# Meta tokens left out behind the mLSTM's state, groups of 256 in the second layer, and a pair's two states block-diagonal in one matrix

## The chip, the cores and the metric

The kernel runs on one core of a Trainium2 chip. The metric is the device time of one execution in microseconds (us). The kernel before takes 3135.82 us (median of three runs, 3132.17 to 3137.7).

## The reference

A trunk of two layers works on 1040 tokens of width 1024: 16 learned meta tokens are set ahead of 1024 input tokens. Each layer is norm, token mixer, residual add, norm, squared-ReLU MLP (1024 to 4096 to 1024), residual add. Layer 0 mixes with a gated DeltaNet, layer 1 with an mLSTM. The output drops the 16 meta tokens again.

The mLSTM has 8 heads, with keys and queries of 64 and values of 128. Cut to what the kernel computes for one head and one chunk of tokens:

```
num   = ec * (q @ C) + (exp(decay) * (q @ k.T)) @ v     # and the same with v = 1 for den
C     = ecl * C + (kw * k).T @ v                        # state that the next chunk reads
h     = num / max(|den|, 1);  out = rms_norm(h) * sigmoid(o)
```

A meta token's `num`, its output gate, its share of the output product and its MLP in layer 1 reach no output. Only its key and value do, through the state C.

## The kernel before, in words

Tokens lie along the free axis: hT is 8 tiles of 128 features by 1040 tokens. Every dense product goes through mm3 (L114 to L117), three matmuls of one kind (fp32r, one record each in the profile): high part of weights by high part of activations, high by low, low by high. A stationary weight tile of 128 by 128 meets a moving tile of G = 260 tokens, four groups to 1040.

The second layer has four stages.

- **mLSTM projections.** MLSTM.proj (L1414) makes q, k, v0, v1, so0 and so1 of a pair of heads: six weight tiles, four groups, 24 matmuls each. There are four pairs.
- **mLSTM mix.** MLSTM.mix (L1445) is a generator. While pair p is projected, mix of pair p-1 is woven in: Ctx.weave steps it once at each yield of the dense work, which comes after every 12 matmuls. Tokens are nine chunks: the 16 meta tokens (number 8 in the code, first in the loop) and eight of 128. The products here are of plain fp32, two records to a matmul; only the transposes are one record. Per chunk and head the mix forms q times state (L1536, 64 partitions deep, one head's 129 columns), scores times values (L1539) and the state's update (L1550, 64 columns of weights, output on 64 of 128 partitions). The state of a pair is one tile, head 0 on partitions 0 to 63, head 1 on 64 to 127. ScalarE scales q times state by ec (L1545), VectorE adds scores times values (L1546), ScalarE squares and sums (L1547), VectorE forms the new state (L1555). For the meta chunk there are small scores (L1485), a small value product (L1539, 16 by 16) and small transposes (L1505) as well. PSUM has two buffers for L1536 and L1539, and one for L1550.
- **Output product.** MLSTM.out (L1589) adds the output product to hT in four groups of 260 (ps_mo); the last pair's mix is woven into it.
- **MLP.** Up (Strassen-like products of seven operands, ps_up, groups of 260) writes its activations to DRAM; Down (ps_dn) reads them back and adds to hT. In layer 1 the first half of Down is one group of 504 tokens, the second two of 260 (REAL, L39). ToOut.write (L1259) transposes 4 blocks of 126 tokens and 5 of 104 and writes them out; the last write ends the kernel.

The order of instructions on each engine is set by the framework's scheduler from the program's order; in the profile the two heads' products of a chunk stand apart, with dense matmuls between them.

Of the kernel before, what the change touches and what calls it, by code (L numbers as in the profile page):

```python
# [15 lines left out]
P = 128  # L16
# [21 lines left out]
ALL = [[(0, G), (G, G)], [(2 * G, G), (3 * G, G)]]  # L38
REAL = [[(META, HALF - META)], ALL[1]]  # L39
# [11 lines left out]
def pair(pool):  # L51
    return tuple(pool.tile([P, 2, HALF], F32R, tag=t, name="act_" + t) for t in ("hi", "lo"))
# [869 lines left out]
class Norm:  # L922


    def __init__(self, c, pool, nw, ss=None):
        self.c, self.nc, self.pool, self.nw = c, c.nc, pool, nw
        self.ss = pool.tile([P, T], F32, tag="ss", name="ss") if ss is None else ss
# [13 lines left out]

    def sums(self, hf):

        nc, c = self.nc, self.c
        pc = c.pq.tile([P, 512], F32, tag=c.pq_tag, name="ps_nrm")[:NT, :2 * G // NT]
        for i in range(2 * G // NT):
            t0 = hf * HALF + i * NT
            nc.tensor.matmul(pc[:, i:i + 1], self.ss[:, t0:t0 + NT], c.ones[:, 0:1], start=True, stop=True)
        nc.scalar.activation(c.rt, pc, AF.Sqrt, scale=1.0 / D, bias=c.eps[:NT])
        nc.vector.reciprocal(c.rt, c.rt)  # L950
        self.summed = hf

    def rms(self, hf):

        nc, c = self.nc, self.c
        if self.summed != hf:
            self.sums(hf)
        yield
        r = self.pool.tile([P, 2, G], F32, tag="r", name="nr", bufs=1)
        dg = r.rearrange("p a b -> p (a b)")[:NT].rearrange("p (a b) -> p a b", b=NT)  # L960
        nc.vector.tensor_tensor(dg, bc(c.ident[:NT, :NT], 1, 2 * G // NT), bc(c.rt, 2, NT), op=ALU.mult)
        yield
        for g in range(2):
            pr = c.pq.tile([P, 512], F32, tag=c.pq_tag, name="ps_nrm")[:, :G]
            nc.tensor.matmul(pr, c.ones[:NT], r[:NT, g], start=True, stop=True)
            nc.scalar.copy(r[:, g], pr)
        return r

    def apply(self, hf, pool):
# [6 lines left out]
        ts = slice(hf * HALF, (hf + 1) * HALF)  # L976
# [11 lines left out]
    def combine(self, hf, pool):  # L988
# [8 lines left out]
        ts = slice(hf * HALF, (hf + 1) * HALF)  # L997
        for j in range(KT // 2):
            b, t = (x.rearrange("p (a b) -> p a b", b=G) for x in self.stages())
            hi, lo = (pool.tile([P, 7, G], F32R, tag=n, name=n) for n in ("xhi", "xlo"))  # L1000
            for k, out in ((j, b[:, 0:4:3]), (j + 4, b[:, 1:3])):
                nc.vector.scalar_tensor_tensor(out, c.hT[:, k, ts].rearrange("p (a b) -> p a b", b=G),
                                               self.nw[:, k:k + 1], r, op0=ALU.mult, op1=ALU.mult)
# [13 lines left out]
class Up:  # L1017
# [47 lines left out]
    def evac(self, i, hs, name, ps, tmp):  # L1065
# [3 lines left out]
        def tile(pool, n):  # L1069
            return pool.tile([P, 2, G], F32, tag=n, name="up_" + n)[:, hs]  # L1070
# [28 lines left out]
    def run(self, jobs):  # L1099
# [4 lines left out]
        for ji, (i, parts, before) in enumerate(jobs):  # L1104
# [4 lines left out]
            for u, (name, xi) in enumerate(self.ORDER):  # L1109
# [7 lines left out]
                ps = self.ps.tile([P, 2, 512], F32, tag="pu", name="ps_up")[:, :, :G]  # L1117
# [8 lines left out]
class Down:  # L1126


    def __init__(self, c, w_down, acts, after, spans):
        self.c, self.nc, self.w, self.acts, self.after, self.spans = c, c.nc, w_down, acts, after, spans  # L1130
        self.a, self.pools, self.next = {}, [], []
# [4 lines left out]
    def fetch(self, j):  # L1136
        st = self.c.row(j % 2, "a_st")
# [3 lines left out]
    def load(self, j):  # L1141
# [3 lines left out]
        hi, lo = self.a[j] = pair(self.pools[j // HB % 2])  # L1145
# [6 lines left out]
    def tiles(self, b, dd, parts, last):  # L1152
# [33 lines left out]
def mlp(c, w_up, w_down, norm, spans, sides, xa, st, acts, after, closed):  # L1186


    down = Down(c, w_down, acts, after, spans)
# [49 lines left out]
class ToOut:  # L1239

    TILES = ((126, 4), (104, 5))

# [16 lines left out]
    def write(self, d, hf):  # L1259
        nc, c = self.c.nc, self.c  # L1260
        w, m = self.TILES[hf]
        t0 = (META, HALF)[hf]
        yield
        for i0 in range(0, m, 4):
            n = min(4, m - i0)
            pt = c.pj.tile([P, 4, P], F32, tag="pj", name="ps_fin")[:w, :n]
            for i in range(n):
                a = t0 + (i0 + i) * w
                nc.tensor.transpose(pt[:, i], c.hT[:, d, a:a + w], c.ident)
            ot = self.pool.tile([P, 4, P], F32, tag="ot", name="ot")[:w, :n]  # L1270
            nc.scalar.copy(ot, pt)
            r0 = t0 - META + i0 * w
            nc.sync.dma_start(out=self.out[r0:r0 + n * w, d * P:(d + 1) * P].rearrange("(i p) f -> p i f", p=w),
                              in_=ot)


class MLSTM:

# [19 lines left out]
    def dense(self, whl, g, m=P):  # L1298
        ps = self.c.pj.tile([P, 512], F32, tag="pj", name="ps_m")[:m, :G]
        gs = slice((g % 2) * G, (g % 2 + 1) * G)  # L1300
# [35 lines left out]
    def gates(self):  # L1336
# [34 lines left out]
        nc.scalar.activation(kw, kw, AF.Exp)  # L1371
        nc.vector.tensor_tensor(cm, pc[:META, 2, :, 0], self.lw[:META, :, 2 * GC], op=ALU.add)
# [15 lines left out]
        self.num = g1.tile([P, GC + 1, 2, P + 1], F32, name="num")  # L1388
        nc.gpsimd.memset(self.num[:, GC], 0.0)

    def decay(self, p, hf):
# [7 lines left out]
        if hf == 0:  # L1399
            E0 = self.g2.tile([META, 2, META], F32, tag="E0", name="E0")  # L1400
            for j in range(2):
                nc.sync.dma_start(out=E0[:, j], in_=md[2 * p + j, 2 * GC, :META].partition_broadcast(META))
                nc.vector.scalar_tensor_tensor(E0[:, j], E0[:, j], self.lw[:META, 2 * p + j, 2 * GC:],
                                               c.mneg[:META, :META], op0=ALU.add, op1=ALU.add)
            nc.scalar.activation(E0, E0, AF.Exp)
# [6 lines left out]
        return (E, E0) if hf == 0 else (E,)  # L1412

    def proj(self, p, s, streams, normed):  # L1414
# [8 lines left out]
        for i, ((name, col, sc), gs) in enumerate(work):  # L1423
# [12 lines left out]
            for g in gs:  # L1436
                ps = yield from self.dense(whl, g)
                dst = s[name][:, g // 2, (g % 2) * G:(g % 2 + 1) * G]
# [6 lines left out]
    def mix(self, p, s):  # L1445
        nc, c, g1, g2 = self.nc, self.c, self.g1, self.g2
        E, E0 = s["E"]
        E = [E, self.decay(p, 1)[0]]
# [10 lines left out]
        for hf in range(2):  # L1459
# [3 lines left out]
            for ci, cc in enumerate(chunks(hf)):  # L1463
                m = P if cc < 2 * GC else META
# [3 lines left out]
                nc.vector.tensor_tensor(kw[:m, ci], pt[:m, 0].rearrange("p (h d) -> p h d", h=2),  # L1468
                                        bc(self.kw[:m, 2 * p:2 * p + 2, cc], 2, 64), op=ALU.mult)
                nc.scalar.copy(V[:m, ci, :, 0:P], pt[:m, 1:3])  # L1470
                yield

        def scores(hf):
# [8 lines left out]
            if hf == 0:  # L1482
                pk = [self.pp.tile([META, META], F32, tag="pp", name="mpk0") for _ in range(2)]
                for j, sl in enumerate(self.HEADS):
                    nc.tensor.matmul(pk[j], part("k", 2 * GC, META)[sl], part("q", 2 * GC, META)[sl],  # L1485
                                     start=True, stop=True)
                for j in range(2):
                    nc.vector.tensor_tensor(E0[:, j], E0[:, j], pk[j], op=ALU.mult)
                yield

        def gated(hf):
            n, o0 = GL[hf], GO[hf]
            for j in range(2):
                og = g1.tile([P, XW], F32, tag="mog", name="mog")[:, :n]
                w = c.mlstm_nw[:, 2 * p + j:2 * p + j + 1]
                so = s[f"so{j}"].rearrange("p a b -> p (a b)")[:, hf * XW:hf * XW + n]
# [3 lines left out]
                nc.vector.scalar_tensor_tensor(og[:, o0:], pt.rearrange("p c t -> p (c t)"), w, so[:, o0:],  # L1500
                                               op0=ALU.mult, op1=ALU.mult)
                yield
                if hf == 0:
                    pt = self.pp.tile([P, META], F32, tag="pp", name="mpo3")
                    nc.tensor.transpose(pt, n2[:META, 2 * GC + j, 0:P], c.ident[:META, :META])  # L1505
                    nc.vector.scalar_tensor_tensor(og[:, :META], pt, w, so[:, :META], op0=ALU.mult, op1=ALU.mult)
                    yield
                if p < self.NH // 2 - 1:
                    nc.sync.dma_start(out=self.dram["o"][2 * p + j, :, hf * XW:hf * XW + n], in_=og)
                    continue  # L1510
                for oh in range(hf + 1) if hf else range(2):
                    a, b = max(hf * XW, oh * HALF), min(hf * XW + n, (oh + 1) * HALF)
                    if a >= b:
                        continue
                    hi, lo = (t[:, j, a - oh * HALF:b - oh * HALF] for t in self.o[oh][p])
                    og_ = og[:, a - hf * XW:b - hf * XW]
                    nc.scalar.copy(hi, og_)
                    nc.vector.tensor_tensor(lo, og_, hi.bitcast(F32), op=ALU.subtract)
# [5 lines left out]
        for hf in range(2):  # L1524
            V = self.V[hf]
            nch = GC + (hf == 0)
# [228 lines left out]
```

## Time and profile before

| what | us |
|---|---|
| median of three runs | 3135.82 |
| the profiled execution | 3135.46 |
| its span | 3133.5 |
| TensorE busy in it | 3056.0 |
| VectorE busy | 1944.4 |
| ScalarE busy | 1482.9 |
| from the first ps_m to the first ps_up of layer 1 (mLSTM) | 1883.5 to 2413.7 |
| from there to the first ps_dn of layer 1 (Up) | 2413.7 to 2759.8 |
| from there to the end (Down, writing) | 2759.8 to 3133.5 |

Matmuls are pipelined, so the time of one is longer than the distance between two; what a matmul costs is read from the starts of its neighbours. PEld is the loading of weights, which can run beside a matmul.

### The profile page before, as it was taken

How to read it: one execution, taken by the hardware profiler on the slowest of the kernel's cores; microseconds unless marked ns; L12 is line 12 of the kernel's file. 1: busy time of each engine (PE TensorE's matmuls, PEld its weight loads, DVE VectorE, ACT ScalarE, POOL GpSimd, SP SyncE). 2: the span in 40 equal slices, each digit the busy share in tenths (PEclk: the TensorE clock that was granted, in tenths of full speed). 3: DMA queues.
4: the chain of work that ended last, by engine and by line, in shares of the span. 5: the costliest groups of instructions: out<-in, count | busy, mean ns of one | idle time of the engine just before them, and what ended most of it. 6: DMA issues, size and time to landing. Idle time of an engine off the chain costs nothing.

```text
span 3133.5 us, 65556 instructions
## 1 busy us (share of the span) xinstructions
PE 3056.0 (98%) x26788; PEld 2910.6 (93%) x26788; DVE 1944.4 (62%) x4483; ACT 1482.9 (47%) x3390; POOL 303.6 (10%) x536
## 2 busy tenths in 40 slices
PE   7999999999999998999999999999999899999999
PEld 7899998999999998999999999899889899989998
DVE  6866777787776578665544554323358876654443
ACT  5666667766655345555311124433444555531112
POOL 1333332232322000000000000000000000000000
PEclk9999999999999999999999999999999999999999
DMA  4233333233335723433423222111222443342323
GB/s 106 80 84 88 88 91 89 82 102 93 88 105 161 227 81 114 129 119 106 141 92 102 89 68 69 51 56 58 67 80 82 122 123 110 117 146 76 100 89 101
DMA packets 402220, 310.97 MB, mean 99 GB/s; under 512 B 30175, under 2 KB 366432, under 8 KB 401920
## 3 DMA queue, kind: packets, MB, share of 16 engines
q1 hardware_dynamic: 366320, 272.69, 29.6%
q10 hardware_dynamic: 35600, 34.10, 3.2%
q8 instruction: 211, 3.46, 0.5%
q14 instruction: 89, 0.73, 0.1%
HBM read 248.11 MB, written 58.62 MB: 98 GB/s over the span
## 4 chain that ended last, share of the span: by engine, by line
PE 83%; DVE 7%; DMA 5%; ACT 2%; issue 1%; POOL 1%; SPq 0%; POOLq 0%; DVEq 0%; ACTq 0%
PE ps_dn L115 8%; PE ps_dn L116 8%; PE ps_dn L117 8%; PE ps_up L115 5%; PE ps_up L116 5%; PE ps_up L117 5%; PE ps_in L115 5%; PE ps_in L117 5%; PE ps_in L116 5%; PE ps_m L115 3%; PE ps_m L117 3%; PE ps_m L116 3%; PE ps_out L115 2%; PE ps_out L117 2%; PE ps_out L116 2%
## 5 line engine op out<-in xcount | busy, mean ns | idle before, releaser
L116 PE MATMUL ps_dn<-act_lo,whi 128*128 128x260 f32 (+1 forms) x1792 | 535.2, 299 | 0.0
L115 PE MATMUL ps_dn<-act_hi,whi 128*128 128x260 f32 (+1 forms) x1792 | 534.8, 298 | 0.4 <-DVE up_c L1073 0.3
L117 PE MATMUL ps_dn<-act_hi,wlo 128*128 128x260 f32 (+1 forms) x1792 | 533.2, 298 | 0.0
L115 PE MATMUL ps_up<-xhi,uop 128*128 128x260 f32 x1792 | 512.3, 287 | 19.9 <-DVE up_u L1073 7.8
L117 PE MATMUL ps_up<-xhi,uop 128*128 128x260 f32 x1792 | 509.5, 285 | 6.6 <-DVE uop L1062 6.6
L116 PE MATMUL ps_up<-xlo,uop 128*128 128x260 f32 x1792 | 511.3, 286 | 0.7 <-DVE xlo L1010 0.7
L134 ACT CAST whi<-wraw 128x1024 fp32r<-128x1024 f32 (+1 forms) x248 | 255.8, 1032 | 511.7 <-PE ps_dn L116 363.8
L115 PE MATMUL ps_in<-act_hi,whi 128*128 128x264 f32 (+1 forms) x1536 | 451.7, 294 | 2.2 <-ACT sz L525 1.2
L117 PE MATMUL ps_in<-act_hi,wlo 128*128 128x264 f32 (+1 forms) x1536 | 448.9, 292 | 0.0
L116 PE MATMUL ps_in<-act_lo,whi 128*128 128x264 f32 (+1 forms) x1536 | 446.7, 291 | 0.0
L1166 DVE TENSOR_TENSOR hT<-hT,ps_dn 128x260 f32<-128x260 f32 (+1 forms) x448 | 203.9, 460 | 327.1 <-PE ps_dn L117 326.7
L135 DVE TENSOR_TENSOR wlo<-wraw,whi 128x1024 fp32r<-128x1024 f32 (+1 forms) x248 | 299.9, 1209 | 149.3 <-ACT whi L134 146.8
L115 PEld LDWEIGHTS ps_up<-xhi,uop 128*128 128x128 f32 x1792 | 341.5, 191 | 25.1 <-issue 6.7
L117 PEld LDWEIGHTS ps_up<-xhi,uop 128*128 128x128 f32 x1792 | 342.1, 191 | 7.9 <-DVE uop L1062 7.8
L115 PEld LDWEIGHTS ps_dn<-act_hi,whi 128*128 128x128 f32 x1792 | 336.9, 188 | 11.6 <-DVE up_c L1073 0.5
L117 PEld LDWEIGHTS ps_dn<-act_hi,wlo 128*128 128x128 f32 x1792 | 337.7, 188 | 10.7
L116 PEld LDWEIGHTS ps_dn<-act_lo,whi 128*128 128x128 f32 x1792 | 336.9, 188 | 10.4
L116 PEld LDWEIGHTS ps_up<-xlo,uop 128*128 128x128 f32 x1792 | 342.5, 191 | 1.4 <-DVE xlo L1010 1.4
L115 PEld LDWEIGHTS ps_in<-act_hi,whi 128*128 128x128 f32 x1536 | 291.3, 190 | 6.1 <-ACT sz L525 1.6
L117 PEld LDWEIGHTS ps_in<-act_hi,wlo 128*128 128x128 f32 x1536 | 291.0, 189 | 3.4 <-issue 1.3
L116 PEld LDWEIGHTS ps_in<-act_lo,whi 128*128 128x128 f32 x1536 | 291.5, 190 | 2.3 <-issue 0.4
L115 PE MATMUL ps_m<-act_hi,whi 128*128 128x260 f32 x768 | 224.2, 292 | 4.6 <-ACT mso L1442 4.2
(413 smaller groups left out, 6479.6 us busy)
## 6 DMA issues: line engine op xcount, KB each, us to landing
wraw<-in_gdn_in_dram SPq DMA_DIRECT2D x96, 512.0 KB
wraw<-in_ff_down_dram SPq DMA_DIRECT2D x72, 512.0 KB
a_st<-d_a SPq DMA_DIRECT2D x64, 520.0 KB
d_a<-up_c ACTq DMA_DIRECT2D x88, 260.0 KB
wraw<-in_ff_up_dram SPq DMA_DIRECT2D x42, 512.0 KB
r<-in_ff_up_dram SPq DMA_DIRECT2D x42, 512.0 KB
wraw<-in_gdn_out_dram SPq DMA_DIRECT2D x32, 512.0 KB
wraw<-in_mlstm_in_dram SPq DMA_DIRECT2D x28, 512.0 KB
```

The costliest lines, as they stand in the source:

```text
L115: nc.tensor.matmul(ps, whi, xhi, start=first, stop=False)
L116: nc.tensor.matmul(ps, whi, xlo, start=False, stop=False)
L117: nc.tensor.matmul(ps, wlo, xhi, start=False, stop=last)
L134: nc.scalar.copy(hi, raw)
L135: nc.vector.tensor_tensor(lo, raw, hi.bitcast(F32), op=ALU.subtract)
L1166: nc.vector.tensor_tensor(hT[:, d, t0:t0 + n], hT[:, d, t0:t0 + n], ps, op=ALU.add)
```

## The change

Layer 1 works on tokens 16 to 1039 alone behind the state, in groups of 256 (Down: 512). Norm, Up, Down and the output product take their first token and group size from a pair (t0, g). The projections of q, so0 and so1 leave out the 16 meta tokens of their first group, which so has 244 columns. The mix computes for the meta chunk only its share of the state. The state of a pair is a tile of 128 by 2 by 129 that is zero off the diagonal, so that one matmul of 128 partitions and 258 columns forms q times state of both heads; the update is one matmul of 128 by 258, of which the two diagonal blocks are read. The state's new value is formed by two VectorE instructions of 64 partitions. ToOut writes one tile of four blocks of 128 tokens for each half.

```diff
-ALL = [[(0, G), (G, G)], [(2 * G, G), (3 * G, G)]]
-REAL = [[(META, HALF - META)], ALL[1]]
+ALL = (0, G)
+REAL = (META, SEQ // 4)
...
 class Down:
+        self.t0, g = tokens
+        self.half, self.n = 2 * g, 2 * g if 2 * g <= 512 else g
...
-                for t0, n in self.spans[hf]:
-                    gs = slice(t0 - hf * HALF, t0 - hf * HALF + n)
+                for g0 in range(0, self.half, self.n):
+                    t0, n = self.t0 + hf * self.half + g0, self.n
+                    gs = slice(g0, g0 + n)
...
 class ToOut:
-        w, m = self.TILES[hf]
-        for i0 in range(0, m, 4):
...
+        t0 = META + hf * SEQ // 2
+        pt = c.pj.tile([P, 4, P], F32, tag="pj", name="ps_fin")
+        for i in range(4):
+            nc.tensor.transpose(pt[:, i], c.hT[:, d, t0 + i * P:t0 + (i + 1) * P], c.ident)
...
 class MLSTM:
+        nc.gpsimd.memset(self.kw[:, :, 2 * GC:], 0.0)
...
+        self.C = [g1.tile([P, 2, P + 1], F32, name=f"C{i}") for i in range(2)]
+        for x in self.C:
+            nc.gpsimd.memset(x, 0.0)
...
-        if hf == 0:
-            E0 = self.g2.tile([META, 2, META], F32, tag="E0", name="E0")
...
-                ps = yield from self.dense(whl, g)
+                g0 = META if g == 0 and name[0] in "qs" else 0
+                ps = yield from self.dense(whl, g, g0=g0)
...
-                po = [self.po.tile([P, 2, P + 1], F32, tag="po", name="mpo")[:m] for _ in range(2)]
                 if C is not None:
-                    for j, sl in enumerate(self.HEADS):
-                        nc.tensor.matmul(po[j][:, 0], part("q", cc)[sl], C[sl], start=True, stop=True)
-                for j in range(2):
-                    e = E[hf][:, j, ci] if ci < GC else E0[:, j]
-                    nc.tensor.matmul(po[j][:, 1], e, V[:m, ci, j], start=True, stop=True)
...
+                    pq, po = (self.po.tile([P, 2, P + 1], F32, tag="po", name="mpo") for _ in range(2))
+                    nc.tensor.matmul(pq, part("q", cc), C, start=True, stop=True)
+                    for j in range(2):
+                        nc.tensor.matmul(po[:, j], E[hf][:, j, ci], V[:, ci, j], start=True, stop=True)
+                    for j in range(2):
+                        nc.scalar.activation(num[:, ci, j], pq[:, j], AF.Copy,
+                                             scale=self.ec[:, 2 * p + j, cc:cc + 1])
+                    nc.vector.tensor_tensor(num[:, ci], num[:, ci], po, op=ALU.add)
...
-                pc = self.pc.tile([P, P + 1], F32, tag="pc", name="mpc")
-                for j in range(2):
-                    nc.tensor.matmul(pc[64 * j:64 * j + 64], Kw[hf][:m, ci, j], V[:m, ci, j], start=True, stop=True)
-                Cn = g2.tile([P, P + 1], F32, tag="C", name="Cn")
...
-                    nc.vector.scalar_tensor_tensor(Cn, C, self.ecl[:, p, cc:cc + 1], pc, op0=ALU.mult, op1=ALU.add)
+                pc = self.pc.tile([P, 2, P + 1], F32, tag="pc", name="mpc")
+                nc.tensor.matmul(pc, Kw[hf][:, ci].rearrange("p h d -> p (h d)"), V[:, ci], start=True, stop=True)
+                Cn = self.C[cc % 2]
+                for j, sl in enumerate(self.HEADS):
...
+                        nc.vector.scalar_tensor_tensor(Cn[sl, j], C[sl, j], self.ecl[sl, p, cc:cc + 1], pc[sl, j],
+                                                       op0=ALU.mult, op1=ALU.add)
```

## Rows read from the trace of the kernel before

**Rows 1.** The page: busy time by engine, and the chain's shares.

```profile
PE 3056.0 (98%) x26788; PEld 2910.6 (93%) x26788; DVE 1944.4 (62%) x4483; ACT 1482.9 (47%) x3390; POOL 303.6 (10%) x536
...
PE 83%; DVE 7%; DMA 5%; ACT 2%; issue 1%; POOL 1%; SPq 0%; POOLq 0%; DVEq 0%; ACTq 0%
```

**Rows 2.** Busy time by stretch: mLSTM with projections, then its output product.

```profile
1883.50:2275.50 392.00, 386.24 (x3005) 356.67 (x3004) 143.87 (x349) 161.37 (x384) 12.29 (x11) 0.99 0.21 62
2275.50:2413.70 138.20, 132.94 (x976) 119.41 (x975) 94.71 (x208) 56.91 (x131) 4.21 (x2) 0.96 0.25 75
```

**Rows 3.** Waits of PE from 1880 to 2414: total, times, longest.

```profile
PE ps_m L115 <- ACT mso L1442: 4.2, 4, 1.2
```

**Rows 4.** Timeline of PE, one head's products between dense matmuls.

```profile
2120.29 0.28 PE L117 MATMUL ps_m<-act_hi,wlo 128*128 128x260 f32 x1
2120.50 0.49 PE L1536 MATMUL mpo<-Cn,mq 64*128 64x129 f32 x2
2120.91 0.49 PE L1539 MATMUL mpo<-mV,E 128*128 128x129 f32 x2
...
2121.36 0.28 PE L116 MATMUL ps_m<-act_lo,whi 128*128 128x260 f32 x1
```

**Rows 5.** Timeline of PE, one chunk's state update between dense matmuls.

```profile
2018.79 0.28 PE L117 MATMUL ps_m<-act_hi,wlo 128*128 128x260 f32 x1
2019.00 0.44 PE L1550 MATMUL mpc<-mV,Kw 128*64 128x129 f32 x4
...
2019.60 0.28 PE L116 MATMUL ps_m<-act_lo,whi 128*128 128x260 f32 x1
```

**Rows 6.** Timeline of PE in layer 0: whole-array fp32 products between dense matmuls.

```profile
178.05 0.28 PE L115 MATMUL ps_in<-act_hi,whi 128*128 128x264 f32 x1
178.17 0.59 PE L767 MATMUL pst<-Yw,Kt 128*128 128x256 f32 x2
178.60 0.61 PE L773 MATMUL po<-Y,AB 128*128 128x128 f32 x4
...
179.17 0.29 PE L117 MATMUL ps_in<-act_hi,wlo 128*128 128x264 f32 x1
```

**Rows 7.** Timeline of PE, two of the meta chunk's small bursts.

```profile
2099.05 0.28 PE L117 MATMUL ps_m<-act_hi,wlo 128*128 128x260 f32 x1
2099.26 0.21 PE L1485 MATMUL mpk<-mq,mk 64*16 64x16 f32 x2
...
2099.62 0.28 PE L116 MATMUL ps_m<-act_lo,whi 128*128 128x260 f32 x1
2099.74 0.28 PE L117 MATMUL ps_m<-act_hi,wlo 128*128 128x260 f32 x1
2099.95 0.43 PE L1550 MATMUL mpc<-mV,Kw 16*64 16x129 f32 x2
...
2100.53 0.29 PE L116 MATMUL ps_m<-act_lo,whi 128*128 128x260 f32 x1
```

**Rows 8.** PE by stretch: Down of layer 0 (260), Down of layer 1 (504, 260, 260).

```profile
1600.00:1800.00 200.00, 200.00 (x1671) 1.00 0.30 95
...
2800.00:3000.00 200.00, 200.00 (x1280) 1.00 0.32 99
```

**Rows 9.** The chain of waits at the end of the kernel: start, us, what.

```profile
3127.38 0.59 ACT ot L1271
3127.99 2.62 DMA out_dram<-ot
```

**Rows 10.** Groups in the mLSTM stage: busy, mean ns, idle before, releasers.

```profile
L1545 ACT ACTIVATE num<-mpo,ec 128x129 f32<-128x129 f32 x64 | 23.7, 370 | 62.6 <-PE mpo L1539 54.3 <-PE mpo L1499 8.3
...
L1546 DVE TENSOR_TENSOR num<-num,mpo 128x129 f32<-128x129 f32 x64 | 18.4, 287 | 44.1 <-ACT num L1545 43.6
...
L1555 DVE SCALAR_TENSOR_TENSOR Cn<-Cn,mecl,mpc 128x129 f32<-128x129 f32 x32 | 11.2, 349 | 37.6 <-PE mpo L1536 30.7 <-PE mpc L1550 6.9
L1480 DVE TENSOR_TENSOR E<-E,mpk 128x512 f32<-128x512 f32 x16 | 10.8, 686 | 14.9 <-PE mpk L1477 14.8
```

More of the change, by code (lines that the diff above doesn't have):

```diff
@@ L48, in bc, with pair @@
     return a.broadcast_to(shape)
-def pair(pool):
-    return tuple(pool.tile([P, 2, HALF], F32R, tag=t, name="act_" + t) for t in ("hi", "lo"))
+def pair(pool, n=HALF):
+    return tuple(pool.tile([P, 2, n], F32R, tag=t, name="act_" + t) for t in ("hi", "lo"))
 class Ctx:
@@ L940, in square, with span @@
             nc.vector.tensor_tensor(ss, ss, sq, op=ALU.add)
+    def span(self, hf):
+        t0 = self.t0 + hf * 2 * self.g
+        return slice(t0, t0 + 2 * self.g)
     def sums(self, hf):
         nc, c = self.nc, self.c
[L945 to L950, printed above, removed]
+        n = 2 * self.g // 8
+        pc = c.pq.tile([P, 512], F32, tag=c.pq_tag, name="ps_nrm")[:n, :8]
+        for i in range(8):
+            t0 = self.span(hf).start + i * n
+            nc.tensor.matmul(pc[:, i:i + 1], self.ss[:, t0:t0 + n], c.ones[:, 0:1], start=True, stop=True)
+        self.rt = c.rt[:n]
+        nc.scalar.activation(self.rt, pc, AF.Sqrt, scale=1.0 / D, bias=c.eps[:n])
+        nc.vector.reciprocal(self.rt, self.rt)
         self.summed = hf
@@ L1136, in fetch @@
     def fetch(self, j):
-        st = self.c.row(j % 2, "a_st")
+        st = self.c.row(j % 2, "a_st")[:, :2 * self.half]
         self.nc.sync.dma_start(out=st, in_=self.acts[j // 2][:, j % 2].rearrange("p a b c -> p (a b c)"))
@@ L1144, in load @@
         st = self.next.pop(0)
-        hi, lo = self.a[j] = pair(self.pools[j // HB % 2])
+        hi, lo = self.a[j] = pair(self.pools[j // HB % 2], self.half)
         nc.scalar.copy(hi.rearrange("p a b -> p (a b)"), st)
@@ L1183, in run, with mlp @@
             self.after.half(hf)
-def mlp(c, w_up, w_down, norm, spans, sides, xa, st, acts, after, closed):
-    down = Down(c, w_down, acts, after, spans)
+def mlp(c, w_up, w_down, norm, sides, xa, st, acts, after, closed):
+    down = Down(c, w_down, acts, after, (norm.t0, norm.g))
     n, e = FF // P // 2, 3
@@ L1239 @@
 class ToOut:
-    TILES = ((126, 4), (104, 5))
     def __init__(self, c, st, out):
@@ L1260, in write @@
         nc, c = self.c.nc, self.c
-        w, m = self.TILES[hf]
-        t0 = (META, HALF)[hf]
+        t0 = META + hf * SEQ // 2
         yield
-        for i0 in range(0, m, 4):
[L1265 to L1274, printed above, removed]
+        pt = c.pj.tile([P, 4, P], F32, tag="pj", name="ps_fin")
+        for i in range(4):
+            nc.tensor.transpose(pt[:, i], c.hT[:, d, t0 + i * P:t0 + (i + 1) * P], c.ident)
+        ot = self.pool.tile([P, 4, P], F32, tag="ot", name="ot")
+        nc.scalar.copy(ot, pt)
+        r0 = t0 - META
+        nc.sync.dma_start(out=self.out[r0:r0 + 4 * P, d * P:(d + 1) * P].rearrange("(i p) f -> p i f", p=P), in_=ot)
 class MLSTM:
@@ L1549, in mix @@
-                for j in range(2):
-                    nc.tensor.matmul(pc[64 * j:64 * j + 64], Kw[hf][:m, ci, j], V[:m, ci, j], start=True, stop=True)
-                Cn = g2.tile([P, P + 1], F32, tag="C", name="Cn")
-                if C is None:
-                    nc.scalar.copy(Cn, pc)
-                else:
-                    nc.vector.scalar_tensor_tensor(Cn, C, self.ecl[:, p, cc:cc + 1], pc, op0=ALU.mult, op1=ALU.add)
+                        nc.vector.scalar_tensor_tensor(Cn[sl, j], C[sl, j], self.ecl[sl, p, cc:cc + 1], pc[sl, j],
+                                                       op0=ALU.mult, op1=ALU.add)
@@ L1626, in first_half @@
         def first_half():
-            norm = self.norm = Norm(c, None, nw, c.row(0, "ss"))
+            norm = self.norm = Norm(c, None, nw, c.row(0, "ss"), REAL)
             sq, ring = c.acts.tile([P, 2, HALF], F32, tag="hi", name="nsq3"), []
@@ L1676, in run @@
         for hf in range(2):
-            self.o.append([pair(pools[hf]) for _ in range(n)])
+            self.o.append([pair(pools[hf], 2 * REAL[1]) for _ in range(n)])
         self.o[0][0] = x0
@@ L1723, in trunk @@
         after = ToNorm(c, c.attn_nw[1], s2)
-        mlp(c, ff_up[0], ff_down[0], norm, ALL, ("right", "left"), xa, s1, dram["a"][0], after, nst.close)
+        mlp(c, ff_up[0], ff_down[0], norm, ("right", "left"), xa, s1, dram["a"][0], after, nst.close)
         m = MLSTM(c, mlstm_in[0], mlstm_gate_bias, mlstm_out[0], after.norm.x, mdram)
@@ L1728, in trunk @@
         with nst2, ExitStack() as s3:
-            mlp(c, ff_up[1], ff_down[1], m.norm, REAL, ("left", "right"), m.xa, s3, dram["a"][1], ToOut(c, s3, out[0]),
+            mlp(c, ff_up[1], ff_down[1], m.norm, ("left", "right"), m.xa, s3, dram["a"][1], ToOut(c, s3, out[0]),
                 lambda: None)
```

142 lines of the change are left out of this document (57 added, 85 removed).

## The prediction

> **What bounds the kernel now.** First the page: PE is busy for 3056.0 us of the span of 3133.5, and the chain of waits lies on PE for 83% [rows 1]. Then the busy time by stretch: through the mLSTM PE is busy for 386.24 of 392.00 us and 132.94 of 138.20 [rows 2], though VectorE and ScalarE have more than half of that time free. The waits of PE say the same from the other side: the largest kind there, ps_m behind a sigmoid, is 4.2 us in all [rows 3]. So the sum to make is of PE's own time. But a busy PE is not a PE that streams: in the first stretch weight loading is busy for only 356.67 us [rows 2], which is where I looked next, in the timeline.
>
> **The mix, now.** Between dense matmuls of 260 columns, which start 0.12 us apart, one head's q times state and scores times values stand as a burst. From the start of the dense matmul ahead of it to that of the second one behind it are 2121.36 - 2120.29 = 1.07 us, and two dense starts belong to it, so the burst costs 0.83 us [rows 4]. There are 64 (8 chunks, 2 heads, 4 pairs). The four records of the state's update cost 2019.60 - 2018.79 - 0.24 = 0.57 us [rows 5], 32 times. Together 53.1 + 18.2 = 71.3 us. Whole-array products of the same kind stand in layer 0: a product of 256 columns and two of 128 cost 179.17 - 178.05 - 0.24 = 0.88 us, of which the first takes 0.43 before the next starts [rows 6]. The same 128-column products take 0.11 us a record there, where those of 129 in the mix are 0.2 apart (0.41 us from L1536 to L1539, two records [rows 4]). So it is not the columns that cost in the mix but the changes between half and whole array.
>
> **The mix, after.** One chunk's q times state of both heads (258 columns, whole array) and the two value products are the form of [rows 6], 0.88 us with one per cent more columns 0.89, and the update (258 columns, whole array) is its first part, 0.43 to 0.44. A chunk costs 1.33 us, 32 of them 42.6. Gain 28.7 us. The bounds: nothing gained if the mixed bursts cost as now (0), and 28.7 + 32 x 0.1 = 32 if the bursts merge and the two of a chunk share their way in and out.
>
> A rule speaks against this part: the Trainium skill (TensorE: Matmul & The Clock Gate, "Part 3: Packing small matmuls — row/col tiling") has matmuls on different row or column strips run side by side, so that two halves take the time of one. By it, filling the array with a zero block gives that away: the four records of the update start within 0.37 us of each other and the next dense matmul, and the merged one streams 0.43, so that the sum would lose some 0.06 x 36 = 2 us there. The trace agrees that they overlap, but the burst as a whole costs 0.57, since the way in and out is dearer than the streaming; and the two heads of q times state stand apart and overlap nothing [rows 4, 5]. I go by the bursts.
>
> **The meta chunk.** Four pairs lose, each: two bursts of small scores at 2099.62 - 2099.05 - 0.24 = 0.33; two of the update by head at 2100.53 - 2099.74 - 0.24 = 0.55 [rows 7]; two of the 16 by 16 value product, which has two records in the same surroundings, taken at the same 0.55 less a little, 0.5; two small transposes (L1505), taken at 0.33 as the other small burst. That is 2 x (0.33 + 0.55 + 0.5 + 0.33) = 3.4 us, and one whole-array update of 0.44 comes in its place: 3.0 a pair, 12 in all. Between half of it, if the scheduler had set them beside others anyway, and all. With them go on ScalarE, VectorE, POOL and SP: two loads of decays a pair, their exponentials, copies and squares of 16 rows, one memset. None of these is on PE's path, so nothing is counted for them.
>
> **Columns.** Down of layer 0 has 1671 starts in 200 us: 119.7 ns for 260 columns. In Down of layer 1, 1280 starts in 200 us, a third of them of 504 columns: (200000 - 853 x 119.7) / 427 = 229.3 ns [rows 8]. The line through both has 0.45 ns a column: 117.9 for 256, 233 for 512, 112.5 for 244. Up of layer 1 has 2688 matmuls (16 x 7 x 2 x 4 x 3): 1.8 ns each, 4.8 us. Output product, 768: 1.4. Down: 768 of 504 and 1536 of 260 become 1536 of 512, so 768 x (229.3 + 239.4 - 466) = 2.1 us. The 288 matmuls of 244 columns (three weight tiles, four pairs, 24): 7.2 ns each if the line holds, 2.1 us; nothing if something else sets the distance below 256; no row shows this kind of matmul with fewer columns than 256, and from above the fp32 kind bounds it, two records of 256 columns in 0.43 us [rows 6], some 0.41 for 244. I take the line, whose rows are nearest, and keep the upper end as a rival.
>
> **Norm, writing, tail.** The norm's sums and their spreading have 64 instead of 65 rows, so they become half-array: six bursts that pay about 0.2 us more each, estimated from 0.33 for two tiny records [rows 7]: -1. The writing has 64 transposes for 72: 0.9. At the end two tiles are written for the last block now, and the second waits for the buffer that the first write of 2.62 us holds [rows 9]: from the copy at 3127.38, six microseconds to the end at 3133.5. After, the add of 512 columns (0.69, the VectorE row of that width [rows 10]), four transposes (0.44), a copy of 0.59 and a write of 2.62 follow the last product, some 5.2 us with the latencies, where from the last ps_dn (about 3126.6) it is 6.9 now: 1.7 gained.
>
> **Waits that are new.** The new state now hangs on two VectorE instructions, one behind the other, and both heads' sums on one add. ScalarE today waits 62.6 us for PE before the 64 scalings [rows 10], 1.96 us a chunk; PE gives up 0.91 us a chunk, so about 1 us of slack is left. The chain of a chunk, from the start of q times state: 0.59 until its result [rows 6], two scalings of 0.37, an add of 258 columns between 0.287 and 0.686 (I take 0.42), two state updates of 0.349 [rows 10]: 2.45 us. PE needs 1.33 and twelve dense matmuls, 1.44, until the next: 2.77. It is hidden, by 0.3. PE runs in order, so behind a late q times state the dense matmuls of the projection queue; that is the second rival. I count nothing for it.
>
> **Sum.** 28.7 + 12 + 4.8 + 1.4 + 2.1 + 2.1 - 1 + 0.9 + 1.7 = 52.7 us off the profiled execution's 3135.46 (2 us around its span; 0.4 below the median of the runs): 3082.8, forecast 3083.
>
> **The rivals.**
> 1. The 288 matmuls of 244 columns lose their rate. At the bound of 0.41 each costs 0.29 more, 83 us: 3083 + 2 + 83 = 3168, slower. It decides from 0.12 + 53/288 = 0.30 us a matmul on. For it: every matmul of this kind in the trace has 256 columns or more, so nothing here excludes a step. Against: from 256 to 504 columns one straight line holds, with one record. Chance 0.08.
> 2. The chain through ScalarE and VectorE becomes the bound of the mix. With one weight cast of about 1 us ahead of the scalings, the 0.3 us of cover is gone and 0.7 late, in 32 chunks 22 us: 3105. For it: the small cover. Against: the scheduler may put dense matmuls ahead, and ScalarE has idle time now. Chance 0.1.
> 3. The change doesn't do what it says in the mix: the merged products pay as much on the way in and out, because they alternate with transposes and the scores, which stay half-array. Then the 28.7 is gone: 3111. For it: the scores (L1477) still work on 64 partitions. Against: whole-array products cost 0.88 beside the same dense kind. Chance 0.04.
>
> **How the numbers follow.** The forecast's case has 0.78. Its own range: 3072 if the stretch of 138 us, whose granted clock averages 0.96 [rows 2], loses less to the clock (5.5 us) and bursts merge more; 3097 if half of the meta chunk's 12 and none of the columns' 7 in Up and Down arrive. With the second rival inside and the others out the range is 3068 to 3108. About 0.2% (6 us) can be told from no change: faster 0.9 (the forecast, rivals 2 and 3), slower 0.08, within 0.02.
>
> **What would show it.** The mLSTM stage, 530.2 us from the first ps_m to the first ps_up, should shrink by about 44; Up (346.1) by 5 and Down to the end (373.7) by 4 to 5. In the timeline, dense matmuls around a chunk's whole-array products should stand 0.9 and 0.44 us further apart, and not 0.83 twice and 0.57. Matmuls of 244 columns that start over 0.3 us apart prove the first rival, PE waits for num, the state or ScalarE's scalings of over 10 us the second. If the mLSTM stage shrinks by less than 20 us without either, the prediction's reason is wrong.

## The result, and the profile after

The changed kernel takes 3078.11 us (median of four runs, 3073.61 to 3079.62) against 3136.14 beside it: a ratio of 0.9814, 95% interval 0.9801 to 0.9827, so 58 us less. The forecast was 3083, which is 53 us less. The profiled execution took 3077.17, its span 3075.5.

The page of the changed kernel, busy time and shares of the chain; [rows 1] are those of before.

```profile
PE 3002.4 (98%) x25836; PEld 2848.9 (93%) x25836; DVE 1934.5 (63%) x4393; ACT 1473.1 (48%) x3358; POOL 301.8 (10%) x534
...
PE 84%; DVE 8%; DMA 4%; ACT 2%; POOL 1%; issue 1%; SPq 0%; DVEq 0%; ACTq 0%; POOLq 0%
```

PE is the bound as before; it has 54 us less to do. Busy time by stretch says where. The stretches are projections with mix, output product, Up, Down to the end; columns are the stretch, its length, then busy time of PE, PEld, DVE, ACT and POOL, granted clock, DMA share, GB/s. The first two answer to [rows 2].

```profile
1886.30:2245.20 358.90, 355.26 (x2881) 348.36 (x2880) 146.87 (x332) 159.51 (x370) 10.34 (x7) 0.99 0.23 68
2245.20:2365.90 120.70, 116.38 (x923) 110.64 (x922) 93.04 (x199) 53.54 (x121) 3.27 (x2) 1.00 0.29 86
2365.90:2705.30 339.40, 327.98 (x2710) 323.73 (x2709) 248.62 (x425) 193.81 (x356) 0.00 (x0) 0.99 0.40 122
2705.30:3075.50 370.20, 365.74 (x1602) 294.57 (x1600) 161.62 (x192) 74.86 (x83) 0.00 (x0) 1.00 0.32 98
```

The projections with mix lost 33.1 us of 392.0, the output product with the last mix 17.5 of 138.2, Up 6.7 of 346.1, Down with the writing 3.5 of 373.7. Not all of that is the change's own: the stretches differ in their time at half clock, which the table of the experiments shows. In the first stretch weight loading is now busy for all but 10.5 us, where before 35.3 us were without it. Put in place by the starts around each gap, 26.7 of the 35.3 us stand at a change between a part and the whole of the array, and 3.0 of the 10.5.

One chunk of the mix, timeline of PE, as in [rows 4, 5]:

```profile
2107.88 0.28 PE L118 MATMUL ps_m<-act_hi,wlo 128*128 128x260 f32 x1
2108.00 0.60 PE L1514 MATMUL mpo<-C,mq 128*128 128x258 f32 x2
2108.43 0.61 PE L1516 MATMUL mpo<-mV,E 128*128 128x129 f32 x4
2108.88 0.60 PE L1525 MATMUL mpc<-mV,Kw 128*128 128x258 f32 x2
...
2109.44 0.28 PE L117 MATMUL ps_m<-act_lo,whi 128*128 128x260 f32 x1
```

2109.44 - 2107.88 - 0.24 = 1.32 us for all that a chunk asks of PE; 1.33 was forecast, and 2.23 it was (2 x 0.83 + 0.57). The first product starts 0.12 behind the dense matmul ahead of it, as a dense one would; before the change a half-array product started 0.21 behind.

Matmuls of 244 columns in the projection of q (timeline), and Down of layer 1, where all matmuls have 512 columns (PE by stretch, as in [rows 8]):

```profile
2119.13 0.27 PE L116 MATMUL ps_m<-act_hi,whi 128*128 128x244 f32 x1
...
2119.80 0.38 PE L1514 MATMUL mpo<-C,mq 128*128 128x258 f32 x1
```

```profile
2800.00:3000.00 200.00, 200.00 (x858) 1.00 0.29 90
```

Six starts of 244 columns in 0.67 us are 112 ns each; 200 us over 858 are 233.1 ns for 512. The line through 260 and 504 gave 112.5 and 233. In Up, where all matmuls have 256 columns now, the distance is a little above the line (PE by stretch):

```profile
2450.00:2650.00 200.00, 200.00 (x1687) 1.00 0.39 119
```

200 us over 1687 are 118.6 ns, where the line gave 117.9. The kernel before has 1673 starts of 260 columns in 200 us of its Up, 119.5 ns.

ScalarE's scalings and VectorE's state updates, as in [rows 10] (busy, mean ns, idle before, releasers):

```profile
L1518 ACT ACTIVATE num<-mpo,ec 128x129 f32<-128x129 f32 x64 | 20.4, 365 | 15.9 <-PE mpo L1514 10.0 <-PE mpo L1493 5.3
...
L1531 DVE SCALAR_TENSOR_TENSOR C<-C,mecl,mpc 64x129 f32<-64x129 f32 x64 | 22.2, 347 | 27.5 <-PE mpc L1525 17.4 <-ACT num L1518 8.0 <-PE mpo L1514 1.0
```

The wait of ScalarE for PE fell from 62.6 to 15.9 us: 0.5 us a chunk in place of 1.96, so the cover is thinner. But PE still hardly waits for it: 0.2 us in all for num, nothing for the scalings or the state (its largest waits there are 4.1 us for hT and 2.4 for a sigmoid).

### The profile page after: what moved, and what is told of

The parts are those of the page before. It is cut to its first block, busy times and chain, and to the rows that moved or that the text cites. A ratio compares the mean times of both kernels' runs of the same rounds, so it can differ in the third digit from the quotient of the medians.

```text
span 3075.5 us, 63578 instructions
## 1 busy us (share of the span) xinstructions
PE 3002.4 (98%) x25836; PEld 2848.9 (93%) x25836; DVE 1934.5 (63%) x4393; ACT 1473.1 (48%) x3358; POOL 301.8 (10%) x534
## 4 chain that ended last, share of the span: by engine, by line
PE 84%; DVE 8%; DMA 4%; ACT 2%; POOL 1%; issue 1%; SPq 0%; DVEq 0%; ACTq 0%; POOLq 0%
PE ps_dn L118 8%; PE ps_dn L117 8%; PE ps_dn L116 8%; PE ps_up L116 6%; PE ps_up L117 6%; PE ps_up L118 6%; PE ps_in L118 5%; PE ps_in L116 5%; PE ps_in L117 5%; PE ps_m L116 3%; PE ps_m L117 3%; PE ps_m L118 3%; PE ps_out L116 2%; PE ps_out L117 2%; PE ps_out L118 2%
## 5 line engine op out<-in xcount | busy, mean ns | idle before, releaser
L116 PE MATMUL ps_up<-xhi,uop 128*128 128x260 f32 (+1 forms) x1792 | 509.1, 285 | 21.6 <-DVE up_u L1083 7.1
L118 PE MATMUL ps_up<-xhi,uop 128*128 128x260 f32 (+1 forms) x1792 | 506.5, 283 | 5.1 <-DVE uop L1072 5.1
L117 PE MATMUL ps_up<-xlo,uop 128*128 128x260 f32 (+1 forms) x1792 | 507.6, 283 | 0.7 <-DVE xlo L1020 0.7
L118 PE MATMUL ps_dn<-act_hi,wlo 128*128 128x260 f32 (+1 forms) x1536 | 492.8, 321 | 0.0
L117 PE MATMUL ps_dn<-act_lo,whi 128*128 128x260 f32 (+1 forms) x1536 | 492.3, 320 | 0.0
L116 PE MATMUL ps_dn<-act_hi,whi 128*128 128x260 f32 (+1 forms) x1536 | 490.4, 319 | 0.8 <-DVE up_c L1083 0.7
L1180 DVE TENSOR_TENSOR hT<-hT,ps_dn 128x260 f32<-128x260 f32 (+1 forms) x384 | 194.9, 510 | 326.1 <-PE ps_dn L118 325.7
L117 PEld LDWEIGHTS ps_dn<-act_lo,whi 128*128 128x128 f32 x1536 | 288.7, 188 | 24.4
L116 PEld LDWEIGHTS ps_dn<-act_hi,whi 128*128 128x128 f32 x1536 | 288.8, 188 | 23.9 <-DVE up_c L1083 0.9
L118 PEld LDWEIGHTS ps_dn<-act_hi,wlo 128*128 128x128 f32 x1536 | 289.4, 188 | 21.7
L116 PE MATMUL ps_m<-act_hi,whi 128*128 128x260 f32 (+1 forms) x768 | 223.6, 292 | 2.4 <-ACT mso L1447 2.4
```

Of the source, the lines that this page charges most:

```text
L116: nc.tensor.matmul(ps, whi, xhi, start=first, stop=False)
L117: nc.tensor.matmul(ps, whi, xlo, start=False, stop=False)
L118: nc.tensor.matmul(ps, wlo, xhi, start=False, stop=last)
L1180: nc.vector.tensor_tensor(hT[:, d, t0:t0 + n], hT[:, d, t0:t0 + n], ps, op=ALU.add)
```

## The experiments

Stage lengths tell more than totals here. They run from the first matmul of ps_m, ps_mo, ps_up and ps_dn to that of the next, worked out from each trace's starts. Of the two kernels that were profiled more than once the projections and the output product repeat within 1 us; layer 0, which no edit touches, is between 1876 and 1888 in these traces, and Up moves by 3 to 4.4. The last column has the time at the lower of the clock's two levels (granted clock 0.50, 1.2 GHz) in the projections, the output product and Up. Where PE is busy, such time costs about half of its length; "at full clock" below means a length less that half, an estimate.

| kernel | total (before beside it) | projections + mix | output product + last mix | Up | Down | at half clock |
|---|---|---|---|---|---|---|
| before, two profiles | 3136.1, 3124.3 (one run) | 392.1, 391.3 | 138.2, 138.0 | 346.1, 343.3 | 373.6, 373.7 | 6.8 / 10.2 / 13.7 and 6.8 / 10.2 / 6.8 |
| changed, three profiles | 3078.1, 3077.0 (3134.0), 3073.8 (3132.6) | 358.9, 358.7, 357.9 | 120.7 each | 339.4, 343.8, 341.6 | 370.2, 370.1, 370.1 | 6.8 / 0 / 3.4, 6.8 / 0 / 10.2 and 3.4 / 0 / 3.4 |
| e1b_half_array | 3104.8 (3134.0) | 377.8 | 127.2 | 342.7 | 370.2 | 3.4 / 0 / 3.4 |
| e5_side_by_side | 3103.6 (3134.0) | 368.9 | 135.5 | 341.4 | 370.1 | 6.8 / 13.7 / 6.8 |
| e6_update_half | 3086.7 (3134.0) | 364.1 | 122.4 | 341.0 | 370.2 | 6.8 / 0 / 3.4 |
| e2_two_whole | 3080.9 (3132.4) | 362.1 | 121.2 | 341.5 | 370.1 | 6.8 / 0 / 6.8 |
| e3_meta_work | 3089.0 (3132.4) | 369.0 | 123.4 | 341.8 | 370.2 | 6.8 / 0 / 6.8 |
| e8_diag_alone | 3101.2 (3132.6) | 367.6 | 127.2 | 343.5 | 373.7 | 3.4 / 0 / 3.4 |
| e4_scores_together | 3072.8 (3132.4) | 356.2 | 119.9 | 342.1 | 370.1 | 10.2 / 0 / 13.7 |
| e7_scores_three_pairs | 3071.4 (3132.6) | 356.2 | 121.0 | 339.1 | 370.1 | 10.2 / 0 / 3.4 |

**Undo the diagonal alone (e1b_half_array).** The state keeps its layout; its products and updates are per head again, each head's product in a PSUM tile of its own as in the kernel before. (A first form with both heads in one tile, e1_half_array, gave no time.)

```diff
-                    nc.tensor.matmul(pq, part("q", cc), C, start=True, stop=True)
+                    for j, sl in enumerate(self.HEADS):
+                        nc.tensor.matmul(po[j][:, 0], part("q", cc)[sl], C[sl, j], start=True, stop=True)
...
-                nc.tensor.matmul(pc, Kw[hf][:, ci].rearrange("p h d -> p (h d)"), V[:, ci], start=True, stop=True)
+                for j, sl in enumerate(self.HEADS):
+                    nc.tensor.matmul(pc[sl, j], Kw[hf][:, ci, j], V[:, ci, j], start=True, stop=True)
```

> The changed kernel with one part undone: each head's state product (64 partitions deep, 129 columns) and each head's update (64 columns of weights) are matmuls of their own on half the array again, and the sums of a chunk are two adds as before the change; the diagonal layout of the state, the dropped meta work and all groups stay as in the changed kernel. Theory A (the changes between half and whole array are what the mix paid): 64 bursts of 0.83 and 32 of 0.57 us come back for 32 x 1.32, so +29 us on the changed kernel run beside it; the mLSTM stage grows from 479.6 to about 508. Rival B (the gain comes from fewer columns, the dropped meta work and fewer matmuls of the MLP, and the diagonal matrix only swaps one cost for another): +0 to +8 us.

3104.75 beside 3076.98 for the changed kernel: +27.8, theory A's 29. The mix stages grew by 19 and 6.5 us, 27 at full clock. Rival B falls: about half of the whole gain is the diagonal state, although it multiplies by zeros. The second add per chunk that came back with it isn't the reason: PE idles for 8.7 us in the two stages here and for 8.0 in the changed kernel.

**The diagonal alone on the kernel before (e8_diag_alone).** The same edit the other way round, in the kernel before, with the meta chunk's products left in.

> The kernel before with only the diagonal state: one whole-array state product and one whole-array update a chunk; the meta chunk's own work, all groups and Down as before. Theory A: 32 x (2.24 - 1.32) = 29 us less, and 2 us for the meta chunk's update in one burst, 3136 to 3105; up to 5 us more if the half clock in the last pair's mix goes with the half-array bursts. Rival B: under 8 us.

3101.15 against 3132.61, ratio 0.9891 (0.9871 to 0.9911): 31.5 less. By stages it is 24.1 and 10.9 us less than the mean of before, 28 of these 35 at full clock; Up and Down stay. The other 7 are half clock, mostly the stretch of the last pair's mix, which is gone here; it is told below. So the total lies at the forecast without the clock's share (31), the stages near the one with it (36). From here to the changed kernel beside it (3073.83) are 27.3 us, the share of everything else.

**Whole array, but two matmuls for one (e2_two_whole).**

```diff
+                    for j in range(2):
+                        nc.tensor.matmul(pq[:, j], part("q", cc), C[:, j], start=True, stop=True)
...
+                    nc.tensor.matmul(pc[:, j], Kw[hf][:, ci].rearrange("p h d -> p (h d)"), V[:, ci, j],
+                                     start=True, stop=True)
```

> The changed kernel, but the two merged matmuls of a chunk are two each: state product per head with all 128 partitions and 129 columns, update per head with all 128 columns of weights and 129 columns. Everything works on the whole array, with the same columns in all. Theory A (whole array against half array): records of 0.11 us as in the value products, 4 x 0.11 = 0.44 for 2 x 0.217, so 0 to +1 us, 3078 to 3079. Rival C (the gain is one instruction for two heads: fewer matmuls, fewer weight loads): about half of the 29 us comes back, 3092.

The ratio to before is 0.9836 (0.982 to 0.9851), which overlaps the changed kernel's interval; the totals can't settle 3 us. The stages are 3.6 and 0.5 longer, with as much time at half clock as two of the changed kernel's three profiles, so theory A's 0 to +1 is missed by about 3. Some 1.2 of it is a matter of order: in two pairs the chunk's twelve whole-array records stand among the sixteen of the scores, and both cost 3.23 us (first from 2096.55 to 2100.02, less 0.24) where 1.29 and 1.34 apart would be 2.63. About what the products themselves cost the timeline of its PE is clear: two products of 129 columns on the whole array cost what the merged one of 258 costs.

```profile
2117.24 0.27 PE L116 MATMUL ps_m<-act_hi,whi 128*128 128x244 f32 x1
2117.34 0.61 PE L1515 MATMUL mpo<-C,mq 128*128 128x129 f32 x4
...
2117.91 0.28 PE L118 MATMUL ps_m<-act_hi,wlo 128*128 128x244 f32 x1
```

2117.91 - 2117.24 - 2 x 0.112 = 0.45 us. A whole chunk costs 1.34 us here and 1.32 merged. Rival C, which asked for 14 us, falls: it is not the number of instructions.

**The update alone on half the array (e6_update_half).** Only the last three lines of e1b's diff.

> The changed kernel with only the update by head again (two matmuls with 64 columns of weights, output on 64 of 128 partitions); the state product stays merged on the whole array. Theory A: the update costs 0.57 us alone, and in a burst with whole-array products it drains once more; 36 x 0.13 = 4.7 us slower, up to 10. Theory F (the halves side by side take the time of one): 36 x 0.06 = 2 us faster, 8 us faster if the streaming halves.

3086.65, +9.7 beside the changed kernel (stages +5.4 and +1.7, 7 in all): between theory A's 4.7 and 10, and the other sign than the rule's. One burst of its PE:

```profile
2101.23 0.28 PE L118 MATMUL ps_m<-act_hi,wlo 128*128 128x260 f32 x1
2101.35 0.60 PE L1514 MATMUL mpo<-C,mq 128*128 128x258 f32 x2
2101.79 0.61 PE L1516 MATMUL mpo<-mV,E 128*128 128x129 f32 x4
2102.33 0.44 PE L1526 MATMUL mpc<-mV,Kw 128*64 128x129 f32 x4
2102.70 0.39 PE L116 MATMUL ps_m<-act_hi,whi 128*128 128x260 f32 x1
2102.92 0.29 PE L117 MATMUL ps_m<-act_lo,whi 128*128 128x260 f32 x1
```

The four half-array records take 0.37 us to the next dense matmul, less than 0.43, as the rule says. But they start 0.54 behind L1516, where whole-array ones start 0.45 behind, and behind the dense matmul after them the next one starts 0.22 later in place of 0.12: 2102.92 - 2101.23 - 0.24 = 1.45 us for the chunk in place of 1.32.

**Both heads side by side (e5_side_by_side).** e1b_half_array with two more steps of dense work ahead of each chunk.

> As e1b_half_array, but with two more steps of dense work ahead of each chunk, so that both PSUM buffers are free and the two heads' state products stand next to each other on the two halves of the array. Theory A: a chunk costs one way in and out of the half array for the products and one for the update; in the kernel before the two bursts that hold both heads and the update cost 1.63 us each against 1.32 for the whole array, so +10 us on the changed kernel (up to +20 where the update stands alone). Theory F, a rule of the Trainium skill (TensorE: Matmul & The Clock Gate, Part 3: two halves take the time of one): state products and update in half the streaming, 0.43 us a chunk less, so -14 us. Rival B: 0.

3103.57, +26.6: a miss for every theory as a total. The bursts are as theory A had them, 1.63 us, 2016.02 - 2014.15 - 0.24:

```profile
2014.15 0.28 PE L118 MATMUL ps_m<-act_hi,wlo 128*128 128x260 f32 x1
2014.36 0.49 PE L1517 MATMUL mpo<-C,mq 64*128 64x129 f32 x4
2014.78 0.71 PE L1519 MATMUL mpo<-mV,E 128*128 128x129 f32 x4
2015.42 0.44 PE L1529 MATMUL mpc<-mV,Kw 128*64 128x129 f32 x4
...
2016.02 0.28 PE L117 MATMUL ps_m<-act_lo,whi 128*128 128x260 f32 x1
```

The reader sees each change between half and whole array here: 0.21 in place of 0.12 into the first product, 0.64 for L1519 in place of 0.45, 0.23 in place of 0.12 after the update. Next to each other the two heads' state products take 0.42 us (L1517 to L1519), as one head's 0.41 in [rows 4], so the two do run side by side. But the merged one takes 0.43 as well. The weight loads of the same burst show where the halves lose their lead:

```profile
2014.35 0.30 PEld L1517 LDWEIGHTS mpo<-C,mq 64*128 64x128 f32 x4
2014.78 0.52 PEld L1519 LDWEIGHTS mpo<-mV,E 128*128 128x128 f32 x4
2015.42 0.20 PEld L1529 LDWEIGHTS mpc<-mV,Kw 128*64 128x64 f32 x4
2015.79 0.19 PEld L116 LDWEIGHTS ps_m<-act_hi,whi 128*128 128x128 f32 x1 [0.17 <-issue]
```

At each of the four changes the load begins only when its matmul begins, and isn't hidden. In the changed kernel's chunk the loads run ahead: that of L1525 begins at 2108.77, its matmul at 2108.88.

The price of a change stands cleanest in two orders of the same eight records, both heads' state and value products. In the kernel before some chunks have them as half, whole, half, whole:

```profile
2014.96 0.28 PE L117 MATMUL ps_m<-act_hi,wlo 128*128 128x260 f32 x1
2015.18 0.49 PE L1536 MATMUL mpo<-Cn,mq 64*128 64x129 f32 x2
2015.59 0.49 PE L1539 MATMUL mpo<-mV,E 128*128 128x129 f32 x2
2016.01 0.49 PE L1536 MATMUL mpo<-Cn,mq 64*128 64x129 f32 x2
2016.43 0.49 PE L1539 MATMUL mpo<-mV,E 128*128 128x129 f32 x2
...
2016.87 0.28 PE L116 MATMUL ps_m<-act_lo,whi 128*128 128x260 f32 x1
```

In e1b_half_array some have them as half, half, whole, whole:

```profile
2130.45 0.27 PE L116 MATMUL ps_m<-act_hi,whi 128*128 128x244 f32 x1
2130.65 0.49 PE L1515 MATMUL mpo<-C,mq 64*128 64x129 f32 x4
2131.07 0.71 PE L1517 MATMUL mpo<-mV,E 128*128 128x129 f32 x4
...
2131.73 0.28 PE L118 MATMUL ps_m<-act_hi,wlo 128*128 128x244 f32 x1
```

The first order costs 2016.87 - 2014.96 - 0.24 = 1.67 us, twice the 0.83 of one head; the second 2131.73 - 2130.45 - 2 x 0.112 = 1.06. Two changes fewer, and two heads at a time, are worth 0.6 us.

In the projections the stage of e5 is 10.2 us longer than in the changed kernel (theory A: 24 x 0.31 = 7.4) and 9 shorter than in e1b. The rest of the miss lies in the last pair, 14.8 us: 13.7 us pass at half clock, which costs some 7, and PE waits 3.2 us for activations of the output product (2.4 for one that is read back, 0.8 for the last pair's). That part I had not foreseen. This experiment so weighs the rule on packing in three pairs of four only; by it some 10 us should have gone there (24 x 0.43), and 10 came.

**The meta chunk's work put back (e3_meta_work).** The loads of decays, small scores, 16 by 16 products, copies and small transposes of before, with results that go nowhere.

> The changed kernel with dead work of the meta chunk put back in the mix (its decays, small scores, 16 by 16 value products, copies, squares and small transposes; results go nowhere). The update stays merged. Theory A (small half-array bursts cost PE their way in and out): 8 x (0.33 + 0.52 + 0.33) = 9.4 us, 3087. Rival D (they fit beside other bursts or in waits of PE): under 3 us.

3088.98 against 3132.36, ratio 0.9858 (0.9843 to 0.9873), 11 to 15 us more than the changed kernel by which of its three sets of runs is taken; the stages say 10.5 and 2.7. The bursts themselves are as priced: in its timeline the two records of a 16 by 16 product cost 0.51 us, two small scores 0.33. That is the 9.4. Of the 3 or 4 beyond it some 1.4 stand where the sixteen records of the second call of scores (a pair has two, for four chunks each) fall among a chunk's whole-array products: the bursts with scores, less those products, add up to 17.3 us here and to 15.9 in the changed kernel. The rest I can't assign to rows. Rival D falls.

**The scores' heads together (e4_scores_together, e7_scores_three_pairs).** The trace of the changed kernel shows what is left on half the array. In the first call of a pair the scheduler sets one head's eight records, then dense work, then the other's:

```profile
2086.01 0.28 PE L117 MATMUL ps_m<-act_lo,whi 128*128 128x260 f32 x1
2086.22 1.16 PE L1480 MATMUL mpk<-mq,mk 64*128 64x128 f32 x8
...
2087.53 0.29 PE L116 MATMUL ps_m<-act_hi,whi 128*128 128x260 f32 x1
```

That is 1.28 us twice. With three steps of dense work ahead of the call, both buffers are free and the sixteen records stand in one burst (e7_scores_three_pairs, a little later in its stage):

```profile
2085.79 0.28 PE L118 MATMUL ps_m<-act_hi,wlo 128*128 128x260 f32 x1
2086.00 1.16 PE L1482 MATMUL mpk<-mq,mk 64*128 64x128 f32 x16
...
2087.31 0.28 PE L117 MATMUL ps_m<-act_lo,whi 128*128 128x260 f32 x1
```

```diff
         def scores(hf):
+            for _ in range(3 if p < self.NH // 2 - 1 else 0):
+                yield
```

> The changed kernel with three more steps of dense work ahead of each call of scores, so that both heads' PSUM buffers are free and the 16 records of a call stand in one burst with the heads alternating; in the changed kernel the first call of each pair stands as two bursts of 8, one head each, at 1.28 us, and the second as one of 16 at 1.29. Theory A (heads on the two halves of the array run side by side only when they stand next to each other): four pairs save 1.27 each, -5 us, 3073. Rival E (the halves don't overlap, or the steps delay the mix so that the output product waits): 0 or slower, 3078 to 3083.

> As e4_scores_together, but with the three steps only while the mix is woven into a projection, none in the last pair, where they did not bring the heads together. Theory A: three split calls of scores save 1.27 each and nothing is late in the last pair, 4 to 6 us less than the changed kernel beside it. Rival E (the steps themselves, not the order of the heads, decide): no difference.

The burst of sixteen costs the same 1.28 us as one of eight: here two heads do take the time of one. The projections are 2.3 us shorter than the changed kernel's mean in both. In total e7 has 3071.44 beside 3073.83, e4 a ratio of 0.98 (0.978 to 0.982), e7 0.9803 (0.9787 to 0.982), after_third 0.9811 (0.9794 to 0.9829): all one way, none clear of the other. The three split calls should have saved 3.8 us, and at first sight the stage shows 60% of that. But both e4 and e7 have a stretch of 3.4 us at half clock near 1978 that no profile of the changed kernel has there; at full clock their projections are 4.4 us shorter, which meets the forecast. e7 has the lowest median of all versions tried, by 2 us that only the stage can tell.

**Both kernels once more (before_again, after_again, after_third).**

> The kernel before as it is, for a second profile: span 3133, mLSTM stage 530 us. If the half clock in the last pair's mix (10 us from 2339) belongs to the program, it stands there again, and Up has its two stretches of 7 us; if it is chance, it is elsewhere or gone.

> The changed kernel as it is, beside the others on one chip: 3078 and an mLSTM stage of 480 us by every theory. Its profile shows whether the stretches of half clock stand where they stood: at 1894 and 2419 us, none between 2330 and 2350, where the kernel before had one of 10 us.

> The changed kernel as it is beside e7_scores_three_pairs and e8_diag_alone on one chip: 3077.

They gave 3124.29 (one run; its span is 11 us shorter than the first profile's, 7.6 of it in layer 0 and 2.8 in Up), 3076.98 and 3073.83. Their profiles are for the clock. PE by stretch, the mix of the last pair in the kernel before, its first profile and its second; the last number but two is the granted clock:

```profile
2335.00:2340.00 5.00, 3.84 (x18) 0.89 0.26 79
2340.00:2345.00 5.00, 5.00 (x18) 0.50 0.28 80
```

```profile
2325.00:2330.00 5.00, 3.68 (x19) 1.00 0.23 67
2330.00:2335.00 5.00, 4.92 (x18) 0.53 0.33 99
2335.00:2340.00 5.00, 5.00 (x20) 0.50 0.00 0
```

A stretch of 10.2 us at the lower level, 1.2 GHz, stands behind the same work in both, after PE had been idle for part of it (3.84 and 3.68 us busy of 5). It belongs to the program, and costs some 5 us. In all three profiles of the changed kernel, in e8_diag_alone and in e1b_half_array it is missing; in e5_side_by_side it is back with 13.7 us. Idle time of PE alone doesn't tell them apart: in e8_diag_alone PE idles for 2.1 us between 2307 and 2314.4, in the same stage, and the clock stays. In Up the kernel before has 6.8 us of it near 2460 in both profiles and the changed one 3.4 us near 2419 in all three; a further 6.8 us near Up's end stands in one profile of each, and Up's length moves in part with it (346.1 and 343.3; 343.8 beside 339.4 and 341.6).

## Why the prediction was right

**The diagonal state**, forecast 28.7 us. Undone it costs 27.8, alone it gives 28 at full clock. The price per chunk was met to a hundredth. The reason given, changes between half and whole array, is what e2, e5 and e6 leave standing: whole-array pieces of any number cost about their columns, and a change costs about 0.2 us (one head's burst has four records of 0.11 and two changes, and costs 0.83). The same eight records in two orders, 1.67 and 1.06 us, say it most directly, though in the second order two heads also run at a time. The Trainium skill (TensorEngine Tiling (Array Packing), "Key Properties") states that a change of tiling mode drains TensorE; the starts here fit it, with 0.21 for 0.12 on the way in. The rule of the Trainium skill that I had weighed against the change (TensorE: Matmul & The Clock Gate, Part 3) holds in the scores (sixteen records in the time of eight), for two heads' state products (0.42 us for one head's 0.41) and for the update's four records alone (0.37 us). It loses to the changes when a chunk goes back and forth.

**The meta chunk**, forecast 12: put back but for the update it costs 13, where 9.4 were priced. So this term was some 3 us too small.

**The columns**, forecast 10.4: 244 and 512 columns are on the line (112 and 233.1 ns), which rested on two points until then. 256 columns in Up are not quite: 118.6 ns, 0.9 to 1.1 less than 260 and not 1.8, so of Up's 4.8 us 2.4 to 3 were there to be had. At full clock Up's stage is only about 1 us shorter in the mean of both kernels' profiles; its 6.7 us in the first pair are mostly half clock, 13.7 us against 3.4. Down and the writing gave 3.6 us of 4.7. In the tail, from the last ps_dn to the end, 5.9 us are left, where I summed 5.2 and it was 6.9: the last copy ends at 3072.14 and the span at 3075.5, 3.4 us later, where I had put a write of 2.62.

**The waits**, forecast nothing: PE waits 0.2 us for num and not for the state. The cover was smaller than I reckoned, 0.5 us a chunk of ScalarE's waiting and not 1.

**What was not in the sum** is the clock. The averaged 0.96 of [rows 2] was the sign of the stretch in the last pair's mix; I put it at the end of the range and not into the forecast. It gives about 5 us, the shorter stretch near 2419 in Up 1.7 more. Without them layer 1 is about 49 us shorter at full clock (the mLSTM 45, forecast 44; Up 1; Down and the writing 3.5), where the sum said 52.7. So the mechanism and its largest terms were right, and that 53 came so near to 58 is in part luck: what Up lacked and what the clock gave stand on opposite sides.

Rival 1 is out by its own test, 112 ns where 300 would have decided; rival 2 by PE's waits; rival 3 by 1.32 us a chunk.

## What to carry to other kernels

Where small products alternate with whole-array matmuls, price the changes between half and whole array and not the columns alone: a zero block that makes a product use all 128 rows can be cheaper than two halves. Read it from the starts of the matmuls on both sides of a burst, and look for a share of busy time in which weight loading is idle though PE is not. Where halves are used, keep them next to each other and many at a time, and see in the trace that the scheduler did.

## What the runs showed of the hardware that was not expected

The sixteen records of two heads' scores took as long as eight of one head's when they stood in one burst, 1.28 us. Two heads' state products side by side took as long as one head's (0.42 and 0.41 us), but no less than the merged one on the whole array (0.43): behind a change the weight load begins with its matmul, and four records are too few to make that up.

Half the clock followed half-array work with idle PE between in the last pair's mix, in the same place in two profiles of the kernel before (10.2 us) and in the same stage of e5_side_by_side (13.7 us). e1b_half_array, with the half-array products of e5 in another order, has none there. Order is one thing that differs, PE's idle time another (7.6 us in that stage of e5, 4.2 in e1b); which of them decides is not settled.

fp32r matmuls of fewer than 256 columns showed no step: 244 columns took 112 ns, on the line through 260 and 504; 256 columns took 118.6, a little above it.
